# RoPE and attention scores on one core: store and load pairs issued as halves of 64 rows

## The chip, the cores and the metric

The kernel runs on one NeuronCore of a Trainium2 chip. The metric is the device time of one execution in microseconds (us). Times are medians of repeated runs; the profile is one execution recorded by the hardware profiler.

## The reference

Inputs q and k are float32 of shape (16 batches, 512 positions, 16 heads, 64 dims); cos and sin are (512, 32). Both q and k are rotated, then the scores of every position against every position are formed for each head:

```python
q_rot = np.concatenate([q1 * cos_q - q2 * sin_q, q1 * sin_q + q2 * cos_q], axis=-1)
k_rot = np.concatenate([k1 * cos_q - k2 * sin_q, k1 * sin_q + k2 * cos_q], axis=-1)
scores = np.einsum('bshd,bthd->bsht', q_rot, k_rot)
```

The output is 16 x 512 x 16 x 512 float32, 268 MB; the inputs are 67 MB.

## The kernel before

**Tiling.** The 512 positions are laid out as 128 partitions of `C` = 4 consecutive positions each. Partition p therefore holds positions 4p to 4p+3: in a load of a whole batch each partition takes 16 KB that are contiguous in HBM. A stage i is one batch `b = i // C` and one position c = `i % C` of each partition; there are `NST` = 64 stages. The stage's output is a tile `stage[s]` of 128 partitions x 16 heads x 512 (32 KB per partition, 4 MB in all), and there are three such buffers (`NST_BUFS`).

**One stage.** `rope` multiplies and adds on VectorE, in place in the input buffer `inb[which]` (two buffers of 2 MB for q, two for k). `transposed` turns the rotated rows on TensorE (line 360) and copies them out of PSUM (line 378). `scores` (line 392) does, for each p of `HP` = 8 head pairs, two matmuls (line 409) into a PSUM tile `ps` and an eviction on ScalarE (line 418) into the stage tile. After the last head pair one DMA on SyncE's queue stores the whole tile (line 426).

**Loads.** `load(which, b)` (line 264) fetches one batch of q or k, 2 MB, also on SyncE's queue. From stage 4 on, the q batch `i // C + 2` is loaded at the end of a stage with `i % C == 2`, the k batch `i // C + 3` at the end of one with `i % C == 3` (lines 507 to 510). Since SyncE issues in program order, such a load comes right behind the store of the same stage. Four q batches, those in `RELIEVED` (5, 8, 11 and 14), go mostly over GpSimd's queue instead, in rows 0 to 119 and 120 to 127.

**Order and waits.** `Plan` collects the operations in program order with the keys that each reads and writes. `resolve` (line 38) works out for each operation which semaphore values it must wait for; every DMA has a semaphore named by its last string argument (`sem`), which rises by 16 when it has landed. `emit` then issues each engine's operations in the order of the program. An input buffer has two groups of keys, `rows` ("in") and `rest` ("in rest"); whoever reads the buffer reads both.

Of the kernel before, what the change touches and what calls it, by code (L numbers as in the profile page):

```python
# [7 lines left out]
PE, ACT, DVE, POOL, SP = "PE", "ACT", "DVE", "POOL", "SP"  # L8
# [170 lines left out]
def kernel(  # L179
# [8 lines left out]
    nc = tc.nc  # L188
# [4 lines left out]
    B, S, H, D = q.shape  # L193
    HD = D // 2
    P = 128
    C = S // P
    HP = H // 2
# [8 lines left out]
    dram = {  # L206
        "q": q.rearrange("b (p c) h d -> b p c h d", c=C),
        "k": k.rearrange("b (p c) h d -> b p c h d", c=C),
    }
    o_v = out.rearrange("b (p c) h t -> b c p h t", c=C)  # L210
# [18 lines left out]
    def one(f):  # L229
        def emit():  # L230
            a = f()
            return a, a

        return emit

    def dma(engine, e, dst, src, sem, reads=(), writes=(), also=()):
        plan.add(engine, one(lambda: e.dma_start(dst, src)), reads, writes, sem=sem, also=also)  # L237
# [22 lines left out]
    RELIEVED = {("q", 5): 0, ("q", 8): 1, ("q", 11): 2, ("q", 14): 3}  # L260
    tiny = [0]
    SLOW = 4

    def load(which, b):
        if b >= B:
            return
        t = inb[which][b % 2]
        sem = f"in_{which}{b % 2}"
        rows = [("in", which, b % 2, c) for c in range(C)]
        rest = [("in rest", which, b % 2, c) for c in range(C)]  # L270
        if (which, b) not in RELIEVED:
            dma(SP, nc.sync, t.rearrange("p c (h d) -> p c h d", h=H), dram[which][b], sem, writes=rows + rest)
            return

        n, E, F = 120, C * H * D, C * H * D // 2
        x = RELIEVED[which, b]
        d = dram[which][b]  # L280

        def move_cursor(k):
            y = tiny[0]
            tiny[0] += 1
            src = bass.AP(q.tensor, 512 * y, [(512, k), (64, 2), (1, 2)])
            dst = scratch[:k, 4 * y : 4 * y + 4].rearrange("p (a b) -> p a b", a=2)
            dma(POOL, nc.gpsimd, dst, src, "cursor", writes=[("scratch", y)])

        def halves(lo, hi, keys, sem):
            src = bass.AP(d.tensor, d.offset + lo * E + F, [(E, hi - lo), (-F, 2), (1, F)])  # L290
            v = t[lo:hi]
            dst = bass.AP(v.tensor, v.offset + F, [(v.ap[0][0], hi - lo), (-F, 2), (1, F)])
            dma(POOL, nc.gpsimd, dst, src, sem, writes=keys)

        plan.add(POOL, None, (), rows)
        if x % 2:
            move_cursor(8)
            halves(n, P, rest, f"rest{x}")
        move_cursor(SLOW + 1)
        halves(0, n, rows, f"part{x}")  # L300
        if not x % 2:
            dma(SP, nc.sync, t[n:].rearrange("p c (h d) -> p c h d", h=H), d[n:], sem, writes=rest)
# [9 lines left out]
    def rope(which, n):  # L312
        if n < C:
            x = units[which, n]
            sv, k1, k2 = "p c (g j) -> p c g j", {"j": HD}, {"j": D}
            cs = cos_t.unsqueeze(2).to_broadcast((P, C, 2 * G, HD))
            ss = ss_v.unsqueeze(2).to_broadcast((P, C, G, D))
            pv = part.rearrange("p (c g j) -> p c g j", c=C, j=D)
            x5 = x.rearrange("p c (h x j) -> p c h x j", x=2, j=HD)
            p5 = part.rearrange("p (c h x j) -> p c h x j", c=C, x=2, j=HD)  # L320
            adds = [(x5[:, :, :, y], p5[:, :, :, 1 - y]) for y in range(2)]
        else:
            x = inb[which][n // C % 2][:, n % C]
            sv, k1, k2 = "p (g j) -> p g j", {"j": HD}, {"j": D}
            cs = cos_t[:, n % C].unsqueeze(1).to_broadcast((P, 2 * H, HD))
            ss = ss_v[:, n % C].unsqueeze(1).to_broadcast((P, H, D))
            pv = part.rearrange(sv, **k2)
            x4 = x.rearrange("p (h x j) -> p h x j", x=2, j=HD)
            swapped = bass.AP(part.tensor, part.offset + HD, [part.ap[0], (D, H), (-HD, 2), (1, HD)])
            adds = [(x4, swapped)]  # L330
        xs, xc = x.rearrange(sv, **k2), x.rearrange(sv, **k1)
        keys, more = src_keys(which, n), src_also(which, n)

        def tt(o, a, b, op, reads, writes):
            plan.add(DVE, one(lambda: nc.vector.tensor_tensor(o, a, b, op=op)), reads, writes, also=more)  # L335

        def products():
            tt(pv, xs, ss, mult, keys + ["ss"], ["part"])
            tt(xc, xc, cs, mult, keys + ["cos"], keys)

        def sums():
            for y, z in adds:
                tt(y, y, z, add, keys + ["part"], keys)

        return [products, sums]
# [34 lines left out]
    def stage_of(i):  # L380
        return i % 2 if i < C else (i - 2) % NST_BUFS
# [4 lines left out]
    def ps_of(i, p):  # L386
        m = HP * i + p if i < FIRST else HP * ((i - FIRST) % PERIOD) + p
        if i >= FIRST and m >= HP * PERIOD - 3:
            return (1, 2, 1)[m - (HP * PERIOD - 3)]
        return m % NPS  # L390

    def scores(i, p):
        y, s = ps_of(i, p), stage_of(i)
        ps, st = ps_s[y], stage[s]
        b = i // C
        if b == 0:
            c, hp = divmod(p, 2)
            lhs, rhs = qTb[i % 2][:, C * hp + c], kTb[0][:, 2 * i + hp]
            keys = [("qT", i % 2, C * hp + c)] + [("kT", 0, 2 * i + hp, x) for x in range(C)]
        else:  # L400
            lhs, rhs = qTb[i % 2][:, p], kTb[b % 2][:, p]
            keys = [("qT", i % 2, p)] + [("kT", b % 2, p, x) for x in range(C)]

        def emit():
            done = []
            for r in range(2):
                lo, hi = 64 * r, 64 * r + 64
                done.append(
                    nc.tensor.matmul(out=ps[:, r, :], lhsT=lhs[lo:hi, :], rhs=rhs[lo:hi, :], start=True, stop=True)  # L409
                )  # L410
            return done[0], done[-1]

        plan.add(PE, emit, keys, [("ps", y)])
        so, si = st[:, 2 * p : 2 * p + 2, :], ps
        if b > 0:
            so = so.rearrange("s r (t c) -> s r t c", c=C)
            si = si.rearrange("s r (c t) -> s r t c", c=C)
        plan.add(ACT, one(lambda: nc.scalar.copy(out=so, in_=si)), [("ps", y)], [("st", s, p)])  # L418
        if b == 0 and p % 2 == 1:
            c = p // 2  # L420
            dma(
                SP, nc.sync, o_v[0, c, :, G * i : G * (i + 1)], st[:, G * c : G * (c + 1)], f"out{s}_{c}",
                reads=[("st", s, p - 1), ("st", s, p)],
            )
        elif b > 0 and p == HP - 1:
            dma(SP, nc.sync, o_v[b, i % C], st, f"out{s}", reads=[("st", s, x) for x in range(HP)])

    def tr_act(which, n):
        for g in range(2):
# [2 lines left out]
    def run(ops):  # L432
        for op in ops:
            op()
# [3 lines left out]
    for head, heads in ((0, G), (G, H - G)):  # L438
        load_units("k", head, heads)
        load_units("q", head, heads)  # L440
    load("k", 1)
    load("q", 1)
    plan.add(POOL, one(lambda: nc.gpsimd.memset(ident, 0.0)), (), ["ident"])
    plan.add(
# [3 lines left out]
                out=ident, in_=ident, compare_op=mybir.AluOpType.not_equal, fill=1.0, base=0,  # L448
# [11 lines left out]
    for i in range(C):  # L460
        plan.step = i
        if i < C - 1:
            dve = rope("k", i + 1) + rope("q", i + 1) + rope("k", C + i)
            nxt = [("k", i + 1), ("q", i + 1)]
        else:
            dve = rope("q", C) + rope("k", C + i) + rope("q", C + 1) + rope("k", 2 * C)
            nxt = [("q", C), ("k", C + i)]
# [16 lines left out]
    for i in range(C, NST):  # L484
        plan.step = i
        tr = {}
        if i + 1 < NST:
            tr[1], tr[3] = ("q", i + 1, 0), ("q", i + 1, 1)
        if i + C < NST:
            tr[5], tr[6] = ("k", i + C, 0), ("k", i + C, 1)  # L490
        dve = []
        if i + 2 < NST:
            dve += rope("q", i + 2)
        if i + 1 + C < NST:
            dve += rope("k", i + 1 + C)
        for p in range(HP):
            scores(i, p)
            if p not in tr:
                continue
            if tr[p][0] == "q":  # L500
                run(dve[:1])
                dve = dve[1:]
                transposed(*tr[p], DVE)
            else:
                transposed(*tr[p], ACT)
        run(dve)
        if i % C == C - 2:
            load("q", i // C + 2)
        elif i % C == C - 1:
            load("k", i // C + 3)  # L510

    plan.resolve()
    with tc.tile_critical(), nc.cleanup_on_exit():  # L513
# [33 lines left out]
```

## Time and profile before

| What | Value |
|---|---|
| Median of 3 runs | 797.86 us (797.85 to 798.58) |
| Profiled execution, its own time | 798.9 us |
| Span of the profile (first to last instruction) | 797.1 us |
| Mean granted TensorE clock | 0.931 |
| Moved by DMA | 335.87 MB, mean 421 GB/s |
| HBM read, written | 67.24 MB, 268.44 MB |
| Stores of 4 MB on SyncE's queue | 60 |
| Stores of 1 MB (batch 0) | 16 |
| Loads of 2 MB on SyncE's queue | 15 of k, 11 of q |
| Loads on GpSimd's queue (1.9 MB) | 4 of q |

The profiled execution's own time is 1.8 us longer than its span, and 1.0 us above the median of the runs. In the page, a digit of the rows of slices is the busy share of one fortieth of the span in tenths. A group of instructions shows its busy time and the mean of one, then the idle time of its engine ahead of it and what ended most of it. A DMA issue shows its size and the median time from issue to landing. "SPq" is SyncE as the issuer of DMAs; "q1" is its DMA queue, spread over the 16 DMA engines.

### The profile page before, as it was taken

The page shows a single profiled execution, that of the slowest core. Times are in us where ns is not written, and L with a number is a line of the kernel's source. Part 1 is how long each engine was busy: PE and PEld are TensorE (multiplying, and loading weights), DVE is VectorE, ACT ScalarE, POOL GpSimd, SP SyncE. Part 2 cuts the span into 40 slices and gives each one's busy share as a digit, 9 for nine tenths or more (in the row PEclk, how much of TensorE's full clock was granted, in tenths as well). Part 3 has the DMA queues.
Part 4 walks back from the last instruction along what each step waited for, and adds up shares of the span by engine and source line. Part 5 has one row for each costly group of instructions (what it writes and reads, how often), then busy time and mean ns, then how long its engine had stood idle before and what let it go on. Part 6 is the DMA issues. An engine that isn't in the chain of part 4 may idle for free.

```text
span 797.1 us, 8197 instructions
## 1 busy us (share of the span) xinstructions
PE 684.3 (86%) x3072; PEld 295.4 (37%) x3072; DVE 545.2 (68%) x516; ACT 562.4 (71%) x647; POOL 8.4 (1%) x18
## 2 busy tenths in 40 slices
PE   3989999897989979799797988979989699789960
PEld 2444443343333434344342433334334244334420
DVE  6999988575775868568585767757758488575400
ACT  3978886785767858578585866768667677678860
POOL 0000000000000000100000000000000100000000
PEclk9999999898998989989898999989989899899995
DMA  8999999999999999999999999999999999999995
GB/s 346 420 424 433 429 418 434 426 434 423 430 413 427 435 434 428 439 421 414 426 427 437 432 435 426 419 428 432 428 431 433 432 429 411 428 432 437 430 433 238
DMA packets 18513, 335.87 MB, mean 421 GB/s; under 512 B 2128, under 2 KB 3408, under 8 KB 4432
## 3 DMA queue, kind: packets, MB, share of 16 engines
q1 hardware_dynamic: 16832, 327.42, 96.5%
q0 software_dynamic: 1376, 8.13, 2.4%
q10 hardware_dynamic: 288, 0.13, 0.1%
q8 instruction: 6, 0.10, 0.0%
q14 instruction: 11, 0.09, 0.0%
HBM read 67.24 MB, written 268.44 MB: 421 GB/s over the span
## 4 chain that ended last, share of the span: by engine, by line
DMA 47%; PE 35%; DVE 8%; ACT 6%; issue 1%; ACTq 0%; DVEq 0%; SPq 0%
DMA out_dram<-st 47%; PE ps L409 27%; PE bank L360 9%; ACT st L418 6%; DVE st L335 3%; DVE part L335 2%; DVE k_sb L335 2%; DVE q_sb L335 1%; DMA st<-in_k_dram 1%; DVE kT L378 0%; DVE qT L378 0%; ACTq L110 0%; DVEq L110 0%; SPq L542 0%; SPq L513 0%
## 5 line engine op out<-in xcount | busy, mean ns | idle before, releaser
L418 ACT COPY st<-ps 128x1024 f32<-128x1024 f32 x512 | 495.5, 1018 | 196.7 <-DMA out_dram<-st 103.3
L409 PE MATMUL ps<-kT,qT 64*128 64x512 f32 x2048 | 542.9, 646 | 71.6 <-ACT st L418 71.6
L409 PEld LDWEIGHTS ps<-kT,qT 64*128 64x128 f32 x2048 | 182.0, 195 | 261.0 <-issue 134.2
L378 DVE COPY qT<-bank 128x512 f32<-128x512 f32 x118 | 81.6, 691 | 197.3 <-PE bank L360 197.3
L360 PEld LDWEIGHTS bank<-ident,q_sb 128*128 128x128 f32 x480 | 54.7, 150 | 101.5 <-issue 99.5
L360 PE MATMUL bank<-ident,q_sb 128*128 128x128 f32 x480 | 85.5, 305 | 1.0 <-DVE q_sb L335 1.0
L360 PEld LDWEIGHTS bank<-ident,k_sb 128*128 128x128 f32 x480 | 50.4, 141 | 94.5 <-DVE k_sb L335 43.1
L360 PE MATMUL bank<-ident,k_sb 128*128 128x128 f32 x480 | 78.6, 287 | 1.6 <-DVE k_sb L335 0.8
L378 ACT COPY kT<-bank 128x512 f32<-128x512 f32 x122 | 72.5, 597 | 6.7 <-PE bank L360 6.7
L335 DVE TENSOR_TENSOR part<-q_sb,ss_t 128x1024 f32<-128x1024 f32 x60 | 73.5, 1225 | 3.2
L335 DVE TENSOR_TENSOR k_sb<-k_sb,part 128x1024 f32<-128x1024 f32 x60 | 73.5, 1225 | 2.1
L335 DVE TENSOR_TENSOR k_sb<-k_sb,cos_t 128x1024 f32<-128x1024 f32 x60 | 73.5, 1225 | 2.0
L335 DVE TENSOR_TENSOR q_sb<-q_sb,cos_t 128x1024 f32<-128x1024 f32 x60 | 73.5, 1225 | 2.1
L335 DVE TENSOR_TENSOR part<-k_sb,ss_t 128x1024 f32<-128x1024 f32 x60 | 73.0, 1216 | 0.3
L335 DVE TENSOR_TENSOR q_sb<-q_sb,part 128x1024 f32<-128x1024 f32 x60 | 72.9, 1216 | 0.0
L360 PE MATMUL bank<-ident,st 128*128 128x128 f32 x64 | 10.8, 319 | 13.2 <-DVE st L335 13.2
L360 PEld LDWEIGHTS bank<-ident,st 128*128 128x128 f32 x64 | 8.2, 161 | 18.5 <-DVE st L335 16.7
L335 DVE TENSOR_TENSOR part<-st,ss_t 128x1024 f32<-128x1024 f32 x8 | 9.8, 1222 | 6.4 <-DMA st<-in_k_dram 6.0
L335 DVE TENSOR_TENSOR st<-st,part 128x512 f32<-128x512 f32 x16 | 11.1, 691 | 0.5
L237 POOL DMA_DIRECT2D scratch<-in_q_dram x6 | 3.6, 600 | 615.4 <-PE bank L360 615.4
L335 DVE TENSOR_TENSOR st<-st,cos_t 128x1024 f32<-128x1024 f32 x8 | 9.8, 1225 | 0.3
L378 ACT COPY qT<-bank 128x512 f32<-128x512 f32 x10 | 5.7, 615 | 3.5 <-PE bank L360 3.5
(11 smaller groups left out, 11.0 us busy)
## 6 DMA issues: line engine op xcount, KB each, us to landing
out_dram<-st SPq DMA_DIRECT2D x60, 4096.0 KB, 25.5
k_sb<-in_k_dram SPq DMA_DIRECT2D x15, 2048.0 KB, 27.1
q_sb<-in_q_dram SPq DMA_DIRECT2D x11, 2048.0 KB, 29.2
out_dram<-st SPq DMA_DIRECT2D x16, 1024.0 KB, 13.3
q_sb<-in_q_dram POOLq DMA_DIRECT2D x4, 1920.0 KB, 32.6
st<-in_k_dram SPq DMA_DIRECT2D x1, 1536.0 KB, 9.0
st<-in_q_dram SPq DMA_DIRECT2D x1, 1536.0 KB, 12.2
st<-in_k_dram SPq DMA_DIRECT2D x1, 512.0 KB, 5.0
```

Of the source, the lines that this page charges most:

```text
L237: plan.add(engine, one(lambda: e.dma_start(dst, src)), reads, writes, sem=sem, also=also)
L335: plan.add(DVE, one(lambda: nc.vector.tensor_tensor(o, a, b, op=op)), reads, writes, also=more)
L360: done = [nc.tensor.transpose(bank[:, x, :], srcs[x], ident) for x in range(4)]
L378: plan.add(engine, one(lambda: copy(out=dst, in_=src)), [("bank", m)], keys)
L409: nc.tensor.matmul(out=ps[:, r, :], lhsT=lhs[lo:hi, :], rhs=rhs[lo:hi, :], start=True, stop=True)
L418: plan.add(ACT, one(lambda: nc.scalar.copy(out=so, in_=si)), [("ps", y)], [("st", s, p)])
```

## The change

Where a load follows a store on SyncE's queue, and it is not one of the four relieved ones, both are cut at row 64. The order of issue becomes: store rows 0 to 63, load rows 0 to 63, store rows 64 to 127, load rows 64 to 127. The second halves get semaphores of their own (`out{s}_64`, `in_q0_64` and so on). The first half of a load writes the keys `rows`, the second the keys `rest`. The load is now emitted from within `scores` right after the store, not at the end of the stage's program.

```diff
+    def load_behind(i):
+        if i % C == C - 2 and i // C + 2 < B:
+            return "q", i // C + 2
+        if i % C == C - 1 and i // C + 3 < B:
+            return "k", i // C + 3
+        return None
+
-    def load(which, b):
+    def load(which, b, part_rows=None):
...
         if (which, b) not in RELIEVED:
-            dma(SP, nc.sync, t.rearrange("p c (h d) -> p c h d", h=H), dram[which][b], sem, writes=rows + rest)
+
+            lo, hi = part_rows or (0, P)
+            keys = {0: rows + rest if hi == P else rows, 64: rest}[lo]
+            dma(
+                SP, nc.sync, t[lo:hi].rearrange("p c (h d) -> p c h d", h=H), dram[which][b][lo:hi],
+                sem if lo == 0 else f"{sem}_{lo}", writes=keys,
+            )
             return
...
         elif b > 0 and p == HP - 1:
-            dma(SP, nc.sync, o_v[b, i % C], st, f"out{s}", reads=[("st", s, x) for x in range(HP)])
+            keys, nxt = [("st", s, x) for x in range(HP)], load_behind(i)
+            if nxt is None or nxt in RELIEVED:
+                dma(SP, nc.sync, o_v[b, i % C], st, f"out{s}", reads=keys)
+                if nxt is not None:
+                    load(*nxt)
+                return
+
+            for lo in (0, 64):
+                hi = lo + 64
+                dma(SP, nc.sync, o_v[b, i % C][lo:hi], st[lo:hi], f"out{s}" + "_64" * (lo > 0), reads=keys)
+                load(*nxt, (lo, hi))
...
         run(dve)
-        if i % C == C - 2:
-            load("q", i // C + 2)
-        elif i % C == C - 1:
-            load("k", i // C + 3)
```

## The prediction

> **What bounds the kernel now.** I read the page from the top: spans and engines, then the slices, the DMA queues, the chain, and last the groups and waits that touch SyncE's ring.
>
> ```profile
> span 797.1 us, 8197 instructions
> PE 684.3 (86%) x3072; PEld 295.4 (37%) x3072; DVE 545.2 (68%) x516; ACT 562.4 (71%) x647; POOL 8.4 (1%) x18
> DMA  8999999999999999999999999999999999999995
> DMA packets 18513, 335.87 MB, mean 421 GB/s; under 512 B 2128, under 2 KB 3408, under 8 KB 4432
> q1 hardware_dynamic: 16832, 327.42, 96.5%
> DMA out_dram<-st 47%; PE ps L409 27%; PE bank L360 9%; ACT st L418 6%; DVE st L335 3%; DVE part L335 2%; DVE k_sb L335 2%; DVE q_sb L335 1%; DMA st<-in_k_dram 1%; DVE kT L378 0%; DVE qT L378 0%; ACTq L110 0%; DVEq L110 0%; SPq L542 0%; SPq L513 0%
> ...
> L418 ACT COPY st<-ps 128x1024 f32<-128x1024 f32 x512 | 495.5, 1018 | 196.7 <-DMA out_dram<-st 103.3
> ...
> out_dram<-st SPq DMA_DIRECT2D x60, 4096.0 KB, 25.5
> k_sb<-in_k_dram SPq DMA_DIRECT2D x15, 2048.0 KB, 27.1
> q_sb<-in_q_dram SPq DMA_DIRECT2D x11, 2048.0 KB, 29.2
> ```
>
> All slices but the first and the last have the 16 DMA engines at 90% or more, and SyncE's queue q1 alone takes 96.5% of 16 engines over the whole span. No compute engine is near that: ScalarE sits 103.3 us in front of its evictions until an earlier store has freed a stage buffer. A 4 MB store takes 25.5 us from issue to landing, though 4.19 MB at the mean 421 GB/s are 10.0 us of transfer: there are two to three transfers in the rings at any moment. So the rings set the time; compute waits for them. The windows of one batch each say the same of the steady part (columns: busy us of PE, PEld, DVE, ACT, POOL, then PEclk, DMA share, GB/s):
>
> ```profile
> 228.50:277.00 48.50, 42.46 (x190) 18.16 (x190) 33.10 (x32) 34.08 (x40) 0.00 (x0) 0.93 1.00 431
> 521.00:570.00 49.00, 42.04 (x190) 18.00 (x188) 34.20 (x32) 33.76 (x39) 0.00 (x0) 0.93 1.01 433
> ```
>
> A batch is four stores of 4.19 MB and two loads of 2.10 MB, 20.97 MB; at 431 to 433 GB/s that is 48.5 us, the length of the window. 432 GB/s over 16 engines is 27.0 GB/s each, and the packet records of the trace give the same: a 32 KB packet of a store takes 1.213 us, a 16 KB packet of a load 0.611 us at best (27.0 and 26.8 GB/s). [...]What costs engine time costs span, one to one.
>
> SyncE's own timeline shows the pairs that the change touches:
>
> ```profile
> 380.77 0.33 SPq L237 DMA_DIRECT2D out_dram<-st  x1
> 381.14 1.07 SPq L237 DMA_DIRECT2D q_sb<-in_q_dram  x1
> 398.27 0.33 SPq L237 DMA_DIRECT2D out_dram<-st  x1
> 398.65 0.91 SPq L237 DMA_DIRECT2D k_sb<-in_k_dram  x1
> ```
>
> [...]No 64-row transfer is in this trace. One small sign is: the eight-row load (rows 120 to 127[...]) that SyncE issues at 184 us. Five of its 16 KB packets overlap between 220.06 and 221.85 us, and two of them take 1.058 and 1.242 us instead of 0.611; the three later ones, alone, take 0.611.[...]
>
> **The change, part by part.** Batches are 4 stages i. A load follows the store of stage i with i%4 = 2 (q of batch i//4+2) and i%4 = 3 (k of batch i//4+3). For q these are batches 3 to 15, 13, less the four that go over GpSimd (5, 8, 11, 14): 9. For k, batches 4 to 15: 12. So 21 pairs become halves; the rest, and the first batch, stay.
>
> - *Moved.* Emission of the load goes ahead of the stage's last DVE operations in program order. SyncE's and GpSimd's own order is unchanged, and the TensorE readers that the load waits for are already emitted. Nothing.
> - *Added issues.* Per pair four DMAs for two: by the timeline one more store issue (0.33 us) and one more load issue (0.8 to 1.1 us for a whole load). The next store on SyncE is 10 us away, and the queue waits for ScalarE 714.1 us in all. Hidden; were it not, 21 x 1.4 = 29 us at most.
> - *Added completions.* 42 more DMAs, 16 completion packets each of 0.009 us, so 42 x 0.009 = 0.4 us per engine. One further semaphore wait for VectorE per load and for ScalarE per store: the bytes are there when it looks. Bounds 0 to 1 us.
> - *The store ends later.* Half the load now precedes its second half: by 2.4 us (1.05 MB at 432). ScalarE's refill of that buffer is 2.4 us later. Behind it wait TensorE (ps full) and the next store. But two whole transfers, 19.4 us, are still in the rings and a stage computes in 10 us (398.27 to 408.29), so they don't run dry. Nothing.
> - *The rate of the halves.* This is what decides. A pair is 6.29 MB: 14.56 us at 432 GB/s. [...]4.85 + 2.43 + 4.85 + 2.43 us become twice that, 29.1 us: 14.56 more. 21 x 14.56 = 306 us. Bounds: [...]0 to 306. [...]The completions of a DMA's 16 engines lie 4 to 6 us apart in the records, but the leading half of them within 0.4 us[...].[...] I take it as nearly in step, 0.4 us off per pair: 21 x 14.16 = 297 us.
>
> The profiled execution is 798.9 us (span 797.1), 1.0 above the median of the runs, 797.86. 798.9 + 297 = 1096, against the median 1095. ScalarE's wait for stores should take it all: 103 + 297 = 400 us.
>
> **The rivals.**
> *Half of it.* [...]The first leaves the loads' 2 x 2.43 = 4.85 us per pair, 21 x 4.85 = 102: 900 us.[...]
> *Nothing of it.* [...]Then only the completions are left, about 1 us: 799.[...]
> *Faster.* The load packets average 0.635 us and not 0.611[...]. All of it is 3344 x 0.024 / 16 = 5 us, for 21 of 26 loads 4: 794.[...]
>
> **How the numbers follow.** [...](1000 to 1105, likeliest 1095): 0.6. Half (815 to 1000, likeliest 900): 0.22. Nothing: 0.12, of which 0.07 within 0.2% (1.6 us, about what a measurement of this kernel can tell) and 0.05 just slower. Faster: 0.06. Slower in all 0.87. The range that keeps 8 in 10 takes the first case and the upper part of the second: 840 to 1110.
>
> **What would show it.** DMA busy stays at 9 in every slice while GB/s falls from 430 to about 270 in batches with two pairs (20.97 MB in 77.6 us) and stays 430 in the last two, where there are no loads; issue to landing of the half stores well above 25 us; "ACT st <- DMA out_dram" near 400 us. 32 KB packets near 2.4 us and 16 KB ones near 1.2 within halves[...]. I am wrong if GB/s stays above 420 in a window with two pairs.

## The result: 22% slower, and the profile after

| | Median | Profiled execution, span |
|---|---|---|
| Before | 798.46 us (797.85 to 799.19, 6 runs) | 797.1 us |
| Changed | 979.25 us (965.44 to 989.55, 6 runs) | 974.2 us |

The ratio is 1.2175 (95% interval 1.211 to 1.224). Here and below a ratio leaves out runs more than 1.5% above the fastest of the same kernel (three of the six here), so it can lie under the quotient of the medians. The forecast was "slower", 1095 us, with a range of 840 to 1110.

First the page of the changed kernel: the same lines as shown of the kernel before (span, engines, DMA slices and totals, queue q1, chain, ScalarE's evictions, DMA issues), and the row of GB/s by slice. The line numbers are those of the changed kernel: L422 is the matmul of the scores, L431 ScalarE's eviction, L237 the helper that issues every DMA.

```profile
span 974.2 us, 8239 instructions
PE 717.0 (74%) x3072; PEld 304.1 (31%) x3072; DVE 545.2 (56%) x516; ACT 563.4 (58%) x647; POOL 8.4 (1%) x18
DMA  9999999999999989999999999999989999799996
GB/s 359 410 424 438 270 322 357 346 343 356 310 360 320 334 221 299 374 398 342 382 393 351 287 317 419 303 363 282 341 296 307 363 408 304 290 254 425 428 432 265
DMA packets 19185, 335.88 MB, mean 345 GB/s; under 512 B 2800, under 2 KB 4080, under 8 KB 5104
q1 hardware_dynamic: 17504, 327.43, 93.9%
DMA out_dram<-st 60%; PE ps L422 18%; PE bank L373 6%; ACT st L431 5%; SPq L237 3%; DVE part L348 1%; DVE st L348 1%; DVE k_sb L348 1%; DVE q_sb L348 1%; DMA st<-in_k_dram 1%; DVE kT L391 0%; DVE qT L391 0%; ACTq L110 0%; DVEq L110 0%; SPq L561 0%
...
L431 ACT COPY st<-ps 128x1024 f32<-128x1024 f32 x512 | 496.5, 1019 | 371.9 <-DMA out_dram<-st 273.7
...
out_dram<-st SPq DMA_DIRECT2D x39, 4096.0 KB, 34.7
out_dram<-st SPq DMA_DIRECT2D x42, 2048.0 KB, 26.3
k_sb<-in_k_dram SPq DMA_DIRECT2D x24, 1024.0 KB, 31.8
q_sb<-in_q_dram SPq DMA_DIRECT2D x18, 1024.0 KB, 27.2
```

VectorE and ScalarE did the same work in the same time (545.2 us in both, 562.4 and 563.4); TensorE was busy 717.0 us and not 684.3, at a mean granted clock of 0.87 and not 0.931. The DMA engines were as busy as before in nearly every slice and moved the same bytes, but at 345 GB/s and not 421. Only the last full slices, where no loads are left, are back at 425 to 432. ScalarE's wait for stores grew from 103.3 to 273.7 us. Here, where the transfers were the bound already, the busy share stayed, the rate fell by 76 GB/s, and the loss came back as 170.4 us more of waiting for buffers. A 2 MB half store takes as long to land (26.3 us) as a 4 MB whole one did before (25.5).

The time can be booked from the page alone. q1's packets took 96.5% of 797.1 = 769.2 us of 16 engines before and 93.9% of 974.2 = 914.8 after: 145.6 of the 177.1 us are longer packets. The packet records split them: a 32 KB store packet went from 1.218 to 1.413 us on average (7680 x 0.195 / 16 = 94 us), a 16 KB load packet from 0.635 to 0.881 (3344 x 0.246 / 16 = 51 us). In the other 31 us engines had no packet of q1. Which engines, and why, is not shown: the packet records carry no engine number.

### The profile page after: what moved, and what is told of

The parts are those of the page before. It is cut to its first block, busy times and chain, and to the rows that moved or that the text cites. A ratio compares the mean times of both kernels' runs of the same rounds, so it can differ in the third digit from the quotient of the medians.

```text
span 974.2 us, 8239 instructions
## 1 busy us (share of the span) xinstructions
PE 717.0 (74%) x3072; PEld 304.1 (31%) x3072; DVE 545.2 (56%) x516; ACT 563.4 (58%) x647; POOL 8.4 (1%) x18
## 2 busy tenths in 40 slices
DMA packets 19185, 335.88 MB, mean 345 GB/s; under 512 B 2800, under 2 KB 4080, under 8 KB 5104
## 3 DMA queue, kind: packets, MB, share of 16 engines
q1 hardware_dynamic: 17504, 327.43, 93.9%
## 4 chain that ended last, share of the span: by engine, by line
DMA 61%; PE 24%; DVE 5%; ACT 5%; SPq 3%; issue 1%; ACTq 0%; DVEq 0%
DMA out_dram<-st 60%; PE ps L422 18%; PE bank L373 6%; ACT st L431 5%; SPq L237 3%; DVE part L348 1%; DVE st L348 1%; DVE k_sb L348 1%; DVE q_sb L348 1%; DMA st<-in_k_dram 1%; DVE kT L391 0%; DVE qT L391 0%; ACTq L110 0%; DVEq L110 0%; SPq L561 0%
## 5 line engine op out<-in xcount | busy, mean ns | idle before, releaser
L422 PE MATMUL ps<-kT,qT 64*128 64x512 f32 x2048 | 569.2, 670 | 215.5 <-ACT st L431 215.5
L431 ACT COPY st<-ps 128x1024 f32<-128x1024 f32 x512 | 496.5, 1019 | 371.9 <-DMA out_dram<-st 273.7
L422 PEld LDWEIGHTS ps<-kT,qT 64*128 64x128 f32 x2048 | 186.5, 202 | 417.8 <-ACT st L431 281.4
L373 PEld LDWEIGHTS bank<-ident,q_sb 128*128 128x128 f32 x480 | 58.9, 159 | 111.6 <-issue 105.0
L373 PE MATMUL bank<-ident,q_sb 128*128 128x128 f32 x480 | 92.0, 322 | 1.0 <-DVE q_sb L348 1.0
L237 POOL DMA_DIRECT2D scratch<-in_q_dram x6 | 3.6, 600 | 768.1 <-PE bank L373 768.1
## 6 DMA issues: line engine op xcount, KB each, us to landing
out_dram<-st SPq DMA_DIRECT2D x42, 2048.0 KB, 26.3
```

Source lines behind the costliest of these rows:

```text
L373: done = [nc.tensor.transpose(bank[:, x, :], srcs[x], ident) for x in range(4)]
```

## Experiments with the whole kernel

In the expectations "theory" is the prediction's estimate: a half of 64 contiguous rows takes twice the time, whether it is stored or loaded, and a half spread over all rows does not. The trace of the kernel before has no such half and shows neither.

**The same turns, other halves.** Two versions keep four DMAs per pair in the same order, but each reaches all 128 partitions or every second one.

Halves by columns:

```diff
-            for lo in (0, 64):
-                dma(SP, nc.sync, o_v[b, i % C][lo:hi], st[lo:hi], ...)
-                load(*nxt, (lo, hi))
+            for j in (0, 1):      # heads 0-7, then 8-15; load: positions 0-1, then 2-3
+                dma(SP, nc.sync, o_v[b, i % C][:, hs], st[:, hs], ...)
+                load(*nxt, j)
```

> The changed kernel with the same number of DMAs in the same turn, but both halved by columns (8 of 16 heads of a store, 2 of 4 positions of a load), so that each DMA reaches all 128 rows. [...]all of the loss goes, 798 to 803 us. Rival, what costs is turning between stores and loads, or twice as many DMAs: stays near 979 us. Rival, faster by thinning out the loads: 794 us.

Measured: 800.97 us, ratio 1.0026 (1.0012 to 1.0041).

Halves of 64 rows, even partitions and then odd ones:

```diff
-                dma(SP, nc.sync, o_v[b, i % C][lo:hi], st[lo:hi], ...)
+                dma(SP, nc.sync, o_v[b, i % C][j:P:2], st[j:P:2], ...)
...
+            ps = slice(0, P) if part_rows is None else slice(part_rows, P, 2)
...
-                SP, nc.sync, t[lo:hi]..., dram[which][b][lo:hi], ...
+                SP, nc.sync, t[ps]..., dram[which][b][ps], ...
```

> The changed kernel with halves of 64 rows in turn as in the change, but one half is the even partitions and the other the odd ones[...]. Theory[...]: the loss goes, 799 to 803 us, as with the columns. Rival (64 rows as such, or four DMAs for two, or the order of the halves costs): near 979 us.

Measured: 801.87 us, ratio 1.0064 (1.003 to 1.0098). From its page:

```profile
DMA packets 19185, 335.88 MB, mean 421 GB/s; under 512 B 2800, under 2 KB 4080, under 8 KB 5104
...
out_dram<-st SPq DMA_DIRECT2D x39, 4096.0 KB, 26.4
out_dram<-st SPq DMA_DIRECT2D x42, 2048.0 KB, 20.5
```

This is the cleanest control of the study: packets and bytes equal those of the changed kernel figure for figure (19185 packets, the same small ones), there are as many DMAs of the same 64 rows, in the same turns, and yet the rate is 421 GB/s and not 345. What costs is not the number of DMAs, their size, or the turning between stores and loads. It is which 64 partitions a half takes. What is left, 2 us with the columns and 5 us with every second row (2 to 8 by its interval), is the whole price of all the rest.

**One half of the pair at a time.**

```diff
+            for lo in (0, 64):
+                dma(SP, nc.sync, o_v[b, i % C][lo:lo + 64], st[lo:lo + 64], ...)
+            load(*nxt)                       # whole
```

> Only the store of a pair is halved (rows 0..63, then 64..127), the load behind it is whole. [...]stores are two thirds of a pair's bytes, so two thirds of the 181 us: about 920 us. Rival[...]: 799 us. Rival, turning between stores and loads costs: 799 us as well, since nothing is in turn here.

Measured: 1004.88 us, ratio 1.2582 (1.252 to 1.2645). Halving only the store is worse than halving both in turn. That no theory had expected.

```diff
+            dma(SP, nc.sync, o_v[b, i % C], st, ...)        # whole
+            for lo in (0, 64):
+                load(*nxt, (lo, lo + 64))
```

> Only the load of a pair is halved, the store ahead of it is whole. [...]one third of the 181 us, about 859 us. Rival[...]: all of it, near 979 us. Rival, turning between stores and loads costs: 799 us.

Measured: 843.76 us, ratio 1.0342 (1.0281 to 1.0402); its runs spread from 821.53 to 868.23. So reads of SBUF (stores) and writes (loads) are both slowed, which refutes the rival by which halves of stores cost nothing and halves of loads all of it. But by the ratios the two losses are 206 and 27 us (45 by the median), and the change loses 174 (181 by the medians). The first alone is more than that: they don't add.

**Other orders of the four halves.**

```diff
+            for lo in (0, 64):
+                dma(SP, ..., st[lo:lo + 64], ...)
+            for lo in (0, 64):
+                load(*nxt, (lo, lo + 64))
```

> The changed kernel with the same four half DMAs per pair, but in the order store rows 0..63, store rows 64..127, load rows 0..63, load rows 64..127. Theory ([...]taking turns lessens it[...]): the two single losses add up, 206 us of the halved stores and 45 us of the halved loads, about 1050 us, above the 979 of the change. Rival, the order of the halves makes no difference: 979 us. Rival, taking turns is itself a cost: below 979 us.

Measured: 1007.83 us, ratio 1.2548 (1.2495 to 1.2601): as slow as halving the store alone, not 1050. In the kernel, halving the load as well costs nothing that can be told once the store is halved. Taking turns, in itself, saves some 30 us (ratio 1.2175 against 1.2548).

```diff
+                dma(SP, ..., st[lo:lo + 64], ...)
+                load(*nxt, (64 - lo, 128 - lo))
```

Of the two amounts expected, the first is the theory's, for reads and writes without a common limit, the second the rival's, for one limit on both:

> The changed kernel, but each store half is followed by the other half of the load: store 0..63, load 64..127, store 64..127, load 0..63. [...]as the change, 979 us give or take 12. [...]clearly below 979, towards 900 us.

Measured: 977.58 us, ratio 1.2225 (1.2195 to 1.2254); its runs spread from 974.9 to 1017.23. It makes no difference that can be told whether store and load in turn take the same half of the rows or opposite ones (ratio 1.2175 against 1.2225). Nothing points to a limit that reads and writes of the same rows share.

## Experiments with DMAs alone

Three kernels leave out all computation and issue DMAs on SyncE's queue in phases; a phase begins when the one before has landed.

```python
for n, todo in enumerate(phases):
    sem = nc.alloc_semaphore(f"phase{n}")
    for dst, src in todo:
        nc.sync.dma_start(dst, src).then_inc(sem, 16)
    nc.sync.wait_ge(sem, 16 * len(todo))
```

> Leaves out all of the computation: only DMAs on SyncE's queue, in phases, each of which starts when the one before has landed in full. [...]6 whole stores 58 us; the same in halves of 64 rows in turn 117 us; 12 times rows 0..63 alone 117 us; halves in turn after one store of 8 rows[...], well under 100 us; 8 whole loads 39 us, in halves 78 us, rows 0..63 alone (half the bytes) 39 us; 4 whole pairs of store and load 58 us, in turn 117 us, crossed (store rows 0..63, load rows 64..127) 117 us too; pairs halved by columns, all 128 rows each, 58 us. Rival[...]: stores in halves stay at 58 us, pairs in turn 78 us. Rival, more and smaller DMAs cost time: columns as slow as rows, rows 0..63 alone no slower per byte than halves, all excesses small (12 DMAs of some tenths of a us each).

The windows view, one stretch per phase (from:to and length in us, POOL's busy time, PEclk, DMA share, GB/s). In order: stores whole, stores in halves, rows 0 to 63 only, halves after the shift, loads whole, loads in halves, loads of rows 0 to 63 only, pairs whole, in turn, crossed, by columns.

```profile
14.18:72.75 58.57, 0.00 (x0) 1.00 1.00 430
74.33:174.70 100.37, 0.00 (x0) 1.00 0.95 251
176.19:299.12 122.93, 0.00 (x0) 1.00 0.99 205
300.28:406.16 105.88, 0.00 (x0) 1.00 0.92 240
407.50:447.88 40.38, 0.00 (x0) 1.00 0.99 415
449.64:529.13 79.49, 0.00 (x0) 1.00 1.00 211
531.22:572.35 41.13, 0.00 (x0) 1.00 0.99 204
573.77:634.63 60.86, 0.00 (x0) 1.00 0.99 414
636.10:721.86 85.76, 0.00 (x0) 1.00 0.93 293
723.36:810.23 86.87, 0.00 (x0) 1.00 0.92 290
811.44:873.90 62.46, 0.00 (x0) 1.00 0.98 403
```

Rows 0 to 63 alone run at 205 GB/s as a store and 204 as a load, where 128 rows run at 430 and 415: half, in both directions. Contiguous halves also differ from every second row in the addresses they touch in HBM, which could be a rival cause. The third phase speaks against it: it writes the same rows of each output tile in the same order as the second and differs only in the SBUF rows that it reads, and it takes 122.9 us, not 100.4.

Three readings differ from what was expected. Stores in halves took 100.4 us and not 117. In the packet records 93% of the packets in the first eighth of the phase are slow (over 1.8 us, where those of whole stores take 1.22), and 26% in the last eighth. In the third phase, which has no other half, every packet stays slow: the fastest takes 2.41 us. Why the share falls where the two halves alternate was not shown. With a store of eight rows ahead of them the halves took 105.9 us in all, and not well under 100. And pairs in turn lost only 24.9 us in four pairs, 6.2 per pair, not 14.6.

The second set asked how stores and loads combine, and what one pair costs among whole stores, as in the kernel.

> Leaves out all of the computation: DMAs on SyncE's queue in phases as before. (1) 8 stores of 16 rows[...]: 4.19 MB in 39 us[...], 19 if such DMAs are held at half rate for another reason. (2) 4 stores, each as even rows and odd rows of the partitions: 39 us[...], 78[...]. (3) Store 0..63 and load 0..63 in turn, 8 times: as pairs in turn, 86 us. (4) Pairs in turn with half the load bytes: theory A (the reads of the next store go on under the load's writes, the longer of both sets the time, 9.7 us per half pair) 78 us; theory B (behind a load the store isn't slowed at all, only the load is) 8 x (4.85 + 2.43) = 58 us. (5) Pairs in turn with twice the load bytes: A 78 us, B 8 x (4.85 + 9.7) = 116 us. (6) to (10) two whole stores, one pair, two whole stores, 23.07 MB: pair whole 54 us; in turn 64 us; only the store halved 64 us; only the load halved 57 us; both halved but not in turn 68 us.

The same view; phases (1) to (10) in order.

```profile
14.32:55.42 41.10, 0.00 (x0) 1.00 0.99 102
57.02:96.15 39.13, 0.00 (x0) 1.00 1.00 429
97.65:189.17 91.52, 0.00 (x0) 1.00 0.94 275
190.74:270.79 80.05, 0.00 (x0) 1.00 0.98 262
272.22:393.95 121.73, 0.00 (x0) 1.00 0.96 276
395.83:451.78 55.95, 0.00 (x0) 1.00 0.99 412
452.96:517.55 64.59, 0.00 (x0) 1.00 0.99 357
518.84:585.10 66.26, 0.00 (x0) 1.00 0.98 348
586.28:645.61 59.33, 0.00 (x0) 1.00 1.00 389
646.91:715.66 68.75, 0.00 (x0) 1.00 0.97 336
```

16 contiguous rows run at 102 GB/s, half of what 64 do (205) and a quarter of 128 (430), at a DMA share of 0.99. Every second row runs at 429: 64 rows two apart are as good as 128. A single pair among whole stores costs 64.6 - 56.0 = 8.6 us in turn; 21 x 8.6 = 181 us, about the loss of the kernel (174 to 181). The store alone in halves costs 10.3 here (9.8 per pair in the kernel), the load alone 3.4 (1.3 to 2.1), both but not in turn 12.8 (9.7 to 10.0). So here, other than in the kernel, halving the load costs 2.5 us more on top of the store.

Neither theory fits phases (4) and (5) together: half the load bytes 80 us (A 78, B 58), twice the load bytes 122 us (A 78, B 116). A third theory, C, an estimate, was made from these times: there are two sums, and the longer one sets the time. The stores' sum has each store as long as in a phase of its half alone and each load at full rate; the loads' sum has it the other way round. From the phases a half store takes 122.9 / 12 = 10.2 us alone and 58.6 / 12 = 4.9 at full rate, a half load 41.1 / 8 = 5.1 and 40.4 / 16 = 2.5. With twice the load the loads' sum is 8 x (4.9 + 2 x 5.1) = 121 us: 122 measured. With half the load the stores' sum is 8 x (10.2 + 1.3) = 92 us, but 80 were measured. Phase (3), low halves alone, has 8 x (10.2 + 2.5) = 102 by C, and 91.5 were measured (86 expected); pairs in turn have 102 and took 85.8. So where the stores' sum is the longer, C gives too much, and what takes the rest off was not isolated.

The third set tests C where it was not fitted: with 16 rows, for which the theories lie far apart. D is the plain sum: every store and every load as long as alone.

> Leaves out all of the computation: transfers of 16 rows[...] in phases. From the phases before: a store of 16 rows takes 5.1 [...] and 1.2 us at the engine's own rate, a load of 16 rows 2.5 and 0.61. Theory C[...], the longer sum sets the time[...]. Theory D[...]. Theory B, behind a load a store isn't slowed. 8 stores alone: 41 us. 8 loads alone: 20 us. 8 stores and 8 loads in turn: C 8 x 5.7 = 46, D 61, B 30 us. 4 stores, each followed by 2 loads: C 25, D 41, B 25 us. 2 stores, each followed by 4 loads: C 23, D 31, B 23 us. About 1.5 us more for each phase from its first issue to the last landing.

```profile
14.48:55.57 41.09, 0.00 (x0) 1.00 0.97 100
56.90:75.49 18.59, 0.00 (x0) 1.00 0.98 111
77.61:122.67 45.06, 0.00 (x0) 1.00 0.98 139
124.77:150.91 26.14, 0.00 (x0) 1.00 0.96 159
153.06:176.98 23.92, 0.00 (x0) 1.00 0.94 129
```

8 and 8 in turn: 45.1 us (C 46, D 61, B 30). 4 and 8: 26.1 (C 25, D 41, B 25). 2 and 8: 23.9 (C 23, D 31, B 23). C holds at all three ratios and D at none; B falls by the first alone. A, worked out from the same times, would give 41, 20 and 20 us. In the first of them the loads, 18.6 us by themselves, add 4.0 us to the 41.1 of the stores.

## Why the prediction was right, and where its size was wrong

**The bound: right.** Transfers set the time, and what slowed them came out in the span. The forecast signs came, most of them weaker: DMA at 8 or 9 in all but two slices, at a lower rate (293 GB/s in the batch from 301 to 365 us, for a forecast of about 270), 425 to 432 GB/s at the end without loads, ScalarE's wait up (273.7 us, forecast 400). Half stores were to land well above 25 us; 26.3 is hardly that.

**What was costed at nothing: nearly right.** Issues, completions, the later end of the store and the moved emission are all in the kernels with columns and with every second row, at 2 and 5 us over before. One term looked wrong for a moment. A store's issue on SyncE's queue takes up to 4.892 us in the changed kernel against 0.689 before, and SPq has 3% of its chain. With every second row it is at most 1.576 us, so in the kernel the long issues are no cost of the four DMAs. Slow rings alone do not explain them either: pairs by columns, at 403 GB/s with 16 DMAs issued back to back, had issues of up to 4.99 us. What made them long was not shown.

**The rate of a half: right in both directions.** That a half of 64 contiguous rows takes twice the time was an estimate ahead of any run. Measured were 204 GB/s for loads and 205 for stores of rows 0 to 63, where all rows had 415 and 430. The eight-row load that the prediction called a small sign was weak evidence. The durations are as given, but three of the five packets took only 0.611 to 0.640 us though they overlap too. Its times of 220.06 to 221.85 us are by the packet records' own clock, which here is some 11 us ahead of the span's.

**The range held, the likeliest case did not.** It was given 1000 to 1105 us; 979 lies below it and inside the 815 to 1000 of "half of it". That the wide range held is in part luck: it took in a rival's amounts.

**The step that failed: "4.85 + 2.43 + 4.85 + 2.43 us become twice that, 29.1 us: 14.56 more".** Each term doubles by itself, as the phases show (10.2 for 4.9, 5.1 for 2.5), but the terms may not be added: sums of both (theory D) were 61 us where 45.1 were measured. By theory C the stores' extra and the loads' lie in two sums, of which only the longer counts. The stores' sum of a pair is 2 x 10.2 + 2 x 2.5 = 25.4 us and the loads' 2 x 4.9 + 2 x 5.1 = 20.0, so a pair costs 25.4 - 14.8 = 10.6 more, not 14.6. Measured are 8.6. C also agrees with the kernel in that the load's halves cost nothing once the store is halved (1007.83 against 1004.88), though not with the single pair, where they cost 2.5 us: not in turn it costs 12.8 us, between C's 10.6 and the forecast's 14.6.

**The second half of that step: "I take it as nearly in step" was too strict.** Its ground, that the leading half of a DMA's completions lie within 0.4 us, holds in the trace of the kernel before for only six of the first ten whole stores; from the twelfth of the 60 on they lie 1.2 to 1.9 us apart. (All 16 lie 2.7 to 7.9 us apart, not 4 to 6.) Nor is the loss steady in the stores in halves, where the share of slow packets falls from 93% to 26%. In the changed kernel, if all the excess is put down to the halves, a half's store packet is on average 7680 x 0.195 / 2688 = 0.56 us longer, which is 42% of the 2.55 - 1.21 = 1.34 that it is longer where rows 0 to 63 are stored alone. In the kernel with only the store halved it is 71%. So turns do help the halves, by about a seventh of the loss (174 us against 203 not in turn). Why packets lose less with a load in between, and what remains between 10.6 and 8.6 us, was not settled by these runs.

**The rivals.** "Nothing" and "faster" fell: a pair costs 8.6 us more, and the kernels with columns and with every second row, 2 and 5 us over before, show that taking turns alone gains nothing. "Half of it", by which the loads alone pay, had an amount that was close: the time lies at the upper edge of its 815 to 1000. But the kernel with only the store halved, at 1004.88 us, refutes its ground.

## What to carry to other kernels

Before a DMA is cut, ask which partitions each piece takes: a piece of 64 contiguous rows ran at half the rate here, and one of 16 at a quarter, and where the rings are the bound, the span pays. Cut by columns or by every second partition, a pair cost 0.1 and 0.2 us here instead of 8.6. For a sum of transfer costs of this kind keep two columns, one with the stores' extra and one with the loads', and take the longer one; in the phases of several pairs that came out right or up to a fifth too high, where adding both was a quarter or more too high.

## What the runs showed of the hardware beyond what was expected

- Stores of rows 0 to 63 ran at 205 GB/s and of rows 0 to 15 at 102. Loads of 64 rows ran at 204, of 16 rows at 111. Eight stores and eight loads of 16 rows in turn took 45.1 us where the stores alone took 41.1.
- 64 rows with a partition step of 2 ran at 429 GB/s, as fast as 128 contiguous rows (430).
- The mean granted TensorE clock fell from 0.931 to 0.87 in the profiled executions, and a matmul of the scores took 670 ns instead of 646. The lower clock is not what slowed the rings: in the phases without any computation, at 1.00, stores of rows 0 to 63 ran at 205 GB/s. Why it fell was not looked into.
